# Splitting all four blocks of a treated K pair first, and rounding its three sums one by one on ScalarE

## The chip, the cores and the metric

The kernel runs on one core of one Trainium2 chip. The metric is the device time of one execution in microseconds. Before the change three runs took 2540.26, 2540.77 and 2540.88 us, median 2540.77.

## The reference

A decoder trunk of two layers on 256 rows of 2048 columns, in float32: a Mamba-2 mixer, then a SwiGLU feed-forward block (FFN), then differential attention, then a second FFN, with RMS norms around each. The change touches the FFNs alone:

```
def swiglu(h, w_gate, w_up, w_down):
    return (jax.nn.silu(h @ w_gate) * (h @ w_up)) @ w_down
...
D_FF = -(-8 * D_MODEL // (3 * 256)) * 256
```

So each FFN multiplies 256 x 2048 activations with two matrices of 2048 x 5632 and the product with one of 5632 x 2048.

## The kernel before

**Three products for one.** TensorE reads rounded operands (fp32r). To keep float32 accuracy each operand is split: `hi` is the value rounded (ScalarE, L133), `lo` is what the rounding left (VectorE, value minus `hi`, L134). A product is then three matmuls: hi by hi, hi by lo, lo by hi (L238).

**A pair of column blocks.** `pair` (L220) computes two neighbouring blocks of 512 columns for both halves of the rows (t = 0, 1). K runs in steps of 256 ("a K pair"): a step needs four weight blocks of 128 x 512, which SP loads into one tile `raw` (places 0, 1 of the first column block, 2, 3 of the second). A plain K pair takes 2 x 2 x 2 products, 24 matmuls. A *treated* K pair computes the same four 256 x 512 pieces with seven products in place of eight, after Winograd's form of Strassen's scheme, 21 matmuls. It needs seven right-hand operands: three weight blocks, one sum that GpSimd's accumulating DMA makes in place 0 (L247: it adds block 1 to it), and three sums that VectorE makes in place (L261 to L263). It also needs four differences of the activations, the "forms" (`make_form`, L820), which VectorE makes from the activations' two halves and which are split as well (`ff`).

**Products and where they go.** Three of the seven products belong to one output alone and accumulate in its PSUM bank `acc`, beside the plain K pairs' products; the other four ("p1", "p5", "p6", "p7") serve several outputs and accumulate in banks of the transposes' pool, `cp`. After the last treated K pair ScalarE and VectorE combine the `cp` banks (L276 to L280).

**Which K pairs.** In gate and up pairs K pairs 2, 4, 6 of 8 are treated, with a plain one between. In the down product `PARTS` names them. Each FFN has 39 treated K pairs. An FFN goes through its column pairs gate, up, gate, up, and now and then a pair of the down product, for the chunks of activations that are ready. After an up pair the activations (`s`, `sw`, `su`, `sx`: two chunks by two row halves) are scaled on VectorE (L897), transposed on TensorE (`pt_f`, L291) and split (`ah_f` on ScalarE, `al_f` on VectorE): the left-hand operands of the down product.

**What sets the order.** The program is recorded in the order of the code, with some work put off by `later`; a scheduler then orders each engine's instructions by what it reckons to be ready. On the chip each of ScalarE, VectorE and GpSimd does its own in that order. `hi` and `lo` come from rings of four tiles each (`hlB`): a tile is free again when the matmuls that read it are done. `raw` tiles come from a ring of three, in the middle part of an FFN from a second ring as well (`rawm`); a raw tile is free when its last low part is made, and only then does SP load the next block into it.

Of the kernel before, what the change touches and what calls it, by code (L numbers as in the profile page):

```python
# [41 lines left out]
def trunk_kernel(ctx, tc, x_rows, x_cols, vec_cols, vec64, post_rows, lam_rows,  # L42
                 w_zxbc, w_dt, w_so, w_qkv, w_ao,
                 w_g0, w_u0, w_d0, w_g1, w_u1, w_d1, out):
    nc = tc.nc
# [55 lines left out]
    xT_hi, xT_lo = [x[:, :, 0] for x in xT], [x[:, :, 1] for x in xT]  # L101
# [6 lines left out]
    hl = [hlA, 2]  # L108
    seq = [0]
# [5 lines left out]
    def raw_tile():  # L115
        deep[1] += 1
        if deep[0] and deep[1] % 5 in (1, 3):
            return mpool.tile([P, 4, 512], F32, tag="m", name="rawm")
        return rawp.tile([P, 4, 512], F32, tag="raw", name="raw")
# [6 lines left out]
    def prep(raw, scale=None):  # L126
        i = seq[0]
        seq[0] += 1
        w = raw.shape[1]
        hi = hl[0].tile([P, w, 512], F32R, tag="hi", name=f"hi{i}")  # L130
        lo = hl[0].tile([P, w, 512], F32R, tag="lo", name=f"lo{i}")
        if scale is None:
            nc.scalar.copy(hi, raw)  # L133
            nc.vector.tensor_tensor(lo, raw, hi.bitcast(F32), op=ALU.subtract)  # L134
        else:
            for j in range(w):
                nc.scalar.activation(hi[:, j], raw[:, j], AF.Copy, scale=scale[j])  # L137
                nc.vector.scalar_tensor_tensor(lo[:, j], raw[:, j], scale[j], hi[:, j].bitcast(F32),  # L138
                                               op0=ALU.mult, op1=ALU.subtract)
        return hi, lo  # L140
# [14 lines left out]
    def later(k, fn):  # L155
        at = step_no[0] + k
        i = len(deferred)
        while i and deferred[i - 1][0] > at:
            i -= 1
        deferred.insert(i, (at, fn))  # L160

    def tick():
        step_no[0] += 1
        while deferred and deferred[0][0] <= step_no[0]:
            deferred.pop(0)[1]()

# [53 lines left out]
    def pair(blocks, stat, seven, form, done):  # L220

        flush()
        acc = {}
        end = len(blocks) - 1  # L230

        def mm(k, st, hi, lo, last):
            first = k not in acc
            if first:
                acc[k] = (auxp.tile([P, 512], F32, tag="aux", name="cp") if isinstance(k, str) else
                          accp.tile([P, 512], F32, tag="acc", name="acc"))
            for q, (a, b) in enumerate(((st[0], hi), (st[0], lo), (st[1], hi))):
                nc.tensor.matmul(acc[k], a, b, start=first and q == 0, stop=last and q == 2)  # L238

        ss = {}  # L240
        for kp, src in enumerate(blocks):
            raw = raw_tile()
            for c in range(2):
                nc.sync.dma_start(raw[:, 2 * c:2 * c + 2], src[c])
            if kp in seven:

                nc.gpsimd.dma_start(raw[:, 0:1], src[0][:, 1:2], accum_op=ALU.add)  # L247
            if kp not in seven:
                hi, lo = prep(raw)
                for t in range(NT):  # L250
                    for c, e in ((0, 2), (1, 0)):
                        for j in range(2):
                            mm((t, c), stat(kp, j, t), hi[:, e + j], lo[:, e + j], kp == end and j == 1)
                        if kp == end:
                            done(t, c, acc[(t, c)], ss)
                    tick()
                continue
            last = kp == seven[-1]
            hi, lo = prep(raw[:, 1:4])

            nc.vector.tensor_tensor(raw[:, 2], raw[:, 2], raw[:, 0], op=ALU.add)  # L261
            nc.vector.tensor_tensor(raw[:, 3], raw[:, 3], raw[:, 2], op=ALU.add)
            nc.vector.tensor_tensor(raw[:, 1], raw[:, 2], raw[:, 1], op=ALU.subtract)  # L263
            sh, sl = prep(raw)
            mm("p1", stat(kp, 0, 0), hi[:, 1], lo[:, 1], last)
            mm((0, 0), stat(kp, 1, 0), hi[:, 2], lo[:, 2], False)
            mm((0, 1), form(kp, 3), hi[:, 0], lo[:, 0], False)
            tick()
            mm("p6", form(kp, 2), sh[:, 2], sl[:, 2], last)
            mm("p5", form(kp, 0), sh[:, 1], sl[:, 1], last)  # L270
            mm("p7", form(kp, 1), sh[:, 0], sl[:, 0], last)
            mm((1, 0), stat(kp, 1, 1), sh[:, 3], sl[:, 3], False)
            tick()
            if last:
                s1, u, w, x = (t512(n) for n in ("s1", "su", "sw", "sx"))
                nc.scalar.copy(s1, acc["p1"])  # L276
                nc.vector.tensor_tensor(u, acc["p6"], s1, op=ALU.subtract)
                nc.vector.tensor_tensor(w, acc["p5"], u, op=ALU.add)
                nc.vector.tensor_tensor(u, acc["p7"], u, op=ALU.add)
                nc.vector.tensor_tensor(x, acc["p7"], w, op=ALU.add)  # L280
                ss.update({(0, 0): (s1, ALU.add), (0, 1): (w, ALU.add), (1, 0): (u, ALU.subtract), (1, 1): (x, ALU.add)})

    def split(dst_hi, dst_lo, src):
        nc.scalar.copy(dst_hi, src)
        nc.vector.tensor_tensor(dst_lo, src, dst_hi.bitcast(F32), op=ALU.subtract)
# [46 lines left out]
    for k2 in range(KD // 2):  # L332
# [4 lines left out]
        if k2 < 6:  # L337
            if k2 % 2 == 0:
                z0_raw.append(rawp.tile([P, 4, 512], F32, tag="raw", name="raw"))
            ks = slice(k2 % 2 * 2, k2 % 2 * 2 + 2)  # L340
# [460 lines left out]
    def t512(name, shape=(P, 512)):  # L801
        return t5.tile(list(shape), F32, tag="t512", name=name)
# [14 lines left out]
    def xr_tile(name, shape=(P, 2, 512), dtype=F32):  # L817
        return postp.tile(list(shape), dtype, tag="xr", name=name, bufs=4)

    def make_form(dct, key, stat, t512, keep=None):  # L820

        xf = t512("xf", (P, NT, 2, P))
        f = t512("f", (P, 4, P))
        for t in range(NT):
            for j in range(2):
                hi, lo = stat(key, j, t)
                nc.vector.tensor_tensor(xf[:, t, j], hi.bitcast(F32), lo.bitcast(F32), op=ALU.add)
        nc.vector.tensor_tensor(f[:, 0], xf[:, 1, 0], xf[:, 1, 1], op=ALU.subtract)
        nc.vector.tensor_tensor(f[:, 1], xf[:, 1, 0], xf[:, 0, 0], op=ALU.subtract)
        nc.vector.tensor_tensor(f[:, 2], xf[:, 0, 0], f[:, 0], op=ALU.subtract)  # L830
        nc.vector.tensor_tensor(f[:, 3], xf[:, 0, 1], f[:, 2], op=ALU.subtract)
        ff = dct[key] = xr_tile("ff", (P, 4, 2, P), F32R)
        split(ff[:, :, 0], ff[:, :, 1], f)
        if keep:
            nc.sync.dma_start(keep, ff.rearrange("p f h q -> p (f h q)").bitcast(F32))

    def form_of(ff, f):
        return ff[:, f, 0], ff[:, f, 1]
# [19 lines left out]
    def ffn(wg, wu, wd, step, final):  # L858
        acts, gt, forms, keep, dforms = {}, {}, {}, {}, {}
# [13 lines left out]
        def kp_stat(kp, j, t):  # L873
            return x_stat(2 * kp + j, t)

        def kg_stat(kg, j, t):
            hi, lo = lookup(acts, (t, kg // 2))
            return hi[:, kg % 2 * 2 + j], lo[:, kg % 2 * 2 + j]

        def form(kp, f):  # L880
            return form_of(lookup(forms, kp), f)
# [29 lines left out]
                nc.sync.dma_start(xr_d[t][h].rearrange("p (e k) -> p e k", e=2), xr_of[(t, h)])  # L911
        for k, kp in enumerate(SEVEN):
            keep[kp] = dramp.tile([P, 8 * P], F32, name=f"form{step}_{kp}")
            later(1 + 3 * k, lambda kp=kp: make_form(forms, kp, kp_stat, t512, keep[kp]))
        mv([wu[10, k] for k in range(4)], u_stat, u_evac, LAG2)
        def form_later(k, kg):
            later(k, lambda: make_form(dforms, kg, kg_stat, t512))

# [4 lines left out]
        for pi, (part, kgs, two) in enumerate(PARTS):  # L923
# [17 lines left out]
            else:  # L941
# [5 lines left out]
                         mid=lambda: fetch_x(lambda t, h: xr_d[t][h].rearrange("p (e k) -> p e k", e=2)))  # L947

    ffn(w_g0, w_u0, w_d0, 1, False)


# [120 lines left out]
    for hg in range(4):  # L1072
        attention_group(hg)
    out_proj(w_ao, True, True, att, list(range(8)), 2, False, LAG2, t512, load_post(2))
    ffn(w_g1, w_u1, w_d1, 3, True)
    flush()

# [59 lines left out]
```

## Time and profile before

| stretch of the span, us | what runs | TensorE busy | VectorE busy | ScalarE busy | clock |
|---|---|---|---|---|---|
| 0 to 753 | Mamba mixer, start of FFN 1 | 747.2 | 528.1 | 467.5 | 1.00 |
| 753 to 1366 | FFN 1, paired columns | 612.9 | 512.2 | 308.6 | 1.00 |
| 1366 to 1869 | attention, start of FFN 2 | 501.1 | 321.1 | 263.5 | 1.00 |
| 1869 to 2482 | FFN 2, paired columns | 613.0 | 512.8 | 309.4 | 1.00 |
| 2482 to 2537 | last column block, norm, output | 43.5 | 28.4 | 15.7 | 0.93 |

The profiled execution took 2539.5 us, its span is 2537.7 us; the median of the three runs is 2540.77. Engines: PE is TensorE, PEld its weight loads, DVE VectorE, ACT ScalarE, POOL GpSimd, SP the engine that issues loads. L133 is line 133 of the kernel. A row of the timelines gives start and duration in us, engine, line, operation, output<-inputs, shapes, count, and in brackets the idle time before it with what ended it; a row of the groups gives count, busy time, mean ns of one, idle time before. The chain's rows give start, length and what ran.

### The profile page before, as it was taken

Reading aid. Unit: us, or ns where it says so; the run is one execution under the profiler, and the core shown is the slowest. Engines: PE = TensorE matmul, PEld = TensorE weight load, DVE = VectorE, ACT = ScalarE, POOL = GpSimd, SP = SyncE. Lnnn points to the kernel's source line nnn. Section 1 sums busy time; section 2 is a strip of 40 time slices with the busy share of each in tenths; the row PEclk is TensorE's granted clock in tenths of the full one; section 3 lists DMA queues with packets and bytes.
Section 4 is the critical chain, followed back from the end, with each engine's and each line's share of the span. In section 5 each row is a group of like instructions: output and inputs, shape, how many; then the busy total and the mean of one; then the engine's idle time right before and its main releaser. Section 6 shows DMA issues by size and latency. Waiting matters only on the chain.

```text
span 2537.7 us, 31211 instructions
## 1 busy us (share of the span) xinstructions
PE 2517.8 (99%) x11866; PEld 2072.2 (82%) x11866; DVE 1902.6 (75%) x2274; ACT 1364.7 (54%) x1655; POOL 222.4 (9%) x214
## 2 busy tenths in 40 slices
PE   9999999999999999999999999999999999999998
PEld 8877888788888888888888888887888888888886
DVE  6777547777687888977887765566688889878985
ACT  5767556666565454544454654455655454535453
POOL 0111000110110000001001100001100000010002
PEclk9999999999999999999999999999999999999999
DMA  7555555455776776778677544544666966786673
GB/s 287 190 169 182 189 191 198 166 183 177 254 260 210 253 238 210 236 231 243 210 237 246 189 150 166 183 151 156 241 223 201 294 216 208 235 262 213 205 252 146
DMA packets 141366, 536.16 MB, mean 211 GB/s; under 512 B 14176, under 2 KB 30880, under 8 KB 114208
## 3 DMA queue, kind: packets, MB, share of 16 engines
q1 hardware_dynamic: 125584, 502.91, 57.3%
q0 software_dynamic: 15264, 30.94, 6.5%
q8 instruction: 93, 1.52, 0.2%
q14 instruction: 57, 0.47, 0.0%
q10 hardware_dynamic: 368, 0.32, 0.0%
HBM read 516.22 MB, written 17.89 MB: 210 GB/s over the span
## 4 chain that ended last, share of the span: by engine, by line
PE 93%; DVE 2%; ACT 1%; issue 1%; DMA 1%; POOL 0%; SPq 0%; DVEq 0%; ACTq 0%; POOLq 0%
PE acc L238 38%; PE acc L187 34%; PE cp L238 8%; PE acc L212 5%; PE acc L214 2%; DVE lo L134 1%; PE sc L1013 1%; DMA mt<-acum_d 1%; PE pt_f L291 1%; ACT hi L133 1%; PE py L568 1%; PE ptx L661 0%; PE po L1049 0%; PE pc L475 0%; PE pp L1040 0%
## 5 line engine op out<-in xcount | busy, mean ns | idle before, releaser
L134 DVE TENSOR_TENSOR lo<-raw,hi 128x2048 fp32r<-128x2048 f32 (+2 forms) x451 | 848.6, 1888 | 362.4 <-ACT hi L133 353.2
L133 ACT CAST hi<-raw 128x2048 fp32r<-128x2048 f32 (+2 forms) x451 | 699.8, 1557 | 593.9 <-DVE raw L263 195.4
L238 PE MATMUL acc<-hi,xT 128*128 128x512 f32 x1840 | 589.2, 390 | 0.0
L187 PE MATMUL acc<-hi,xT 128*128 128x512 f32 x1792 | 588.9, 399 | 0.0
L238 PEld LDWEIGHTS acc<-hi,xT 128*128 128x128 f32 x1840 | 345.3, 188 | 71.5
L187 PEld LDWEIGHTS acc<-hi,xT 128*128 128x128 f32 x1792 | 335.9, 188 | 73.4 <-issue 4.9
L238 PE MATMUL acc<-lo,xT 128*128 128x512 f32 x920 | 358.1, 389 | 0.0
L187 PE MATMUL acc<-lo,xT 128*128 128x512 f32 x896 | 352.1, 393 | 1.1 <-DVE lo L134 1.1
L133 ACT CAST hi<-rawm 128x2048 fp32r<-128x2048 f32 (+1 forms) x115 | 207.8, 1807 | 173.4 <-DVE rawm L263 108.3
L134 DVE TENSOR_TENSOR lo<-rawm,hi 128x2048 fp32r<-128x2048 f32 (+1 forms) x115 | 248.0, 2157 | 69.9 <-ACT hi L133 66.1
L238 PEld LDWEIGHTS acc<-lo,xT 128*128 128x128 f32 x920 | 172.7, 188 | 35.5
L187 PEld LDWEIGHTS acc<-lo,xT 128*128 128x128 f32 x896 | 169.0, 189 | 38.0 <-DVE lo L134 3.6
L238 PE MATMUL acc<-hi,ah_f 128*128 128x512 f32 x468 | 183.1, 391 | 0.0
L238 PE MATMUL acc<-hi,al_f 128*128 128x512 f32 x468 | 182.1, 389 | 0.0
L238 PE MATMUL acc<-lo,ah_f 128*128 128x512 f32 x468 | 182.1, 389 | 0.0
L212 PE MATMUL acc<-xT,hi 128*128 128x512 f32 x512 | 179.8, 397 | 0.0
L238 PE MATMUL cp<-hi,ff 128*128 128x512 f32 x468 | 156.9, 389 | 0.0
L214 PE MATMUL acc<-xT,lo 128*128 128x256 f32 x512 | 142.6, 280 | 0.0
L138 DVE SCALAR_TENSOR_TENSOR lo<-raw,cols,hi 128x512 fp32r<-128x512 f32 x128 | 92.5, 767 | 57.2 <-ACT hi L137 56.9
L137 ACT ACTIVATE hi<-raw,cols 128x512 fp32r<-128x512 f32 x128 | 84.8, 715 | 58.9 <-PE acc L187 41.4
L212 PEld LDWEIGHTS acc<-xT,hi 128*128 128x128 f32 x512 | 96.1, 188 | 22.6
L238 PEld LDWEIGHTS acc<-hi,al_f 128*128 128x128 f32 x468 | 87.8, 188 | 18.4
(279 smaller groups left out, 3470.4 us busy)
## 6 DMA issues: line engine op xcount, KB each, us to landing
raw<-in_w_zxbc_dram SPq DMA_DIRECT2D x77, 1024.0 KB, 4.8
raw<-in_w_d_dram SPq DMA_DIRECT2D x98, 512.0 KB, 5.9
raw<-in_w_g_dram SPq DMA_DIRECT2D x96, 512.0 KB, 5.9
raw<-in_w_u_dram SPq DMA_DIRECT2D x96, 512.0 KB, 5.8
raw<-in_w_qkv_dram SPq DMA_DIRECT2D x48, 1024.0 KB, 4.8
raw<-in_w_so_dram SPq DMA_DIRECT2D x32, 1024.0 KB, 4.8
rawm<-in_w_g_dram SPq DMA_DIRECT2D x64, 512.0 KB, 5.8
rawm<-in_w_u_dram SPq DMA_DIRECT2D x64, 512.0 KB, 6.0
```

Of the source, the lines that this page charges most:

```text
L133: nc.scalar.copy(hi, raw)
L134: nc.vector.tensor_tensor(lo, raw, hi.bitcast(F32), op=ALU.subtract)
L137: nc.scalar.activation(hi[:, j], raw[:, j], AF.Copy, scale=scale[j])
L138: nc.vector.scalar_tensor_tensor(lo[:, j], raw[:, j], scale[j], hi[:, j].bitcast(F32), op0=ALU.mult, op1=ALU.subtract)
L187: nc.tensor.matmul(acc[t], a, b[:, j], start=(i == 0 and j == 0 and q == 0), stop=(i == last and j == 1 and q == 2))
L212: nc.tensor.matmul(acc[ct], hi[:, j, cs], x.rearrange("p a s -> p (a s)"), start=(i == 0 and j == 0), stop=False)
L214: nc.tensor.matmul(acc[ct][:, :S], lo[:, j, cs], x[:, 0], start=False, stop=(i == last and j == 1))
L238: nc.tensor.matmul(acc[k], a, b, start=first and q == 0, stop=last and q == 2)
L291: nc.tensor.transpose(pt[:, j], src[:, j * P:(j + 1) * P], ident)
L568: nc.tensor.matmul(py[e * 64:(e + 1) * 64, a], xd[c][:, 2 * a + e], mts[c][:, 2 * a + e], start=True, stop=True)
L1013: nc.tensor.matmul(sc[c][:, h], qT[cp, h % 2, ts], kT[cp, h % 2, :nk * P], start=True, stop=True)
```

## The change

In a treated K pair the first split now takes all four raw blocks, sum in place 0 included (before: places 1 to 3), and the second one only the three sums VectorE makes (before: all four places after the sums). ScalarE rounds each sum by an instruction of its own, right behind the VectorE instruction that makes it; the low parts of the three are made by two instructions, of two places and of one. The order of the sums changes with it, and the product "p7", whose operand now belongs to the first split, moves to the first group of matmuls: 12 matmuls read the first split and 9 the second (before 9 and 12). In `make_form` one addition per row half takes two blocks together (before: two additions).

```
-            hi, lo = prep(raw[:, 1:4])
+            hi, lo = prep(raw)
+            sh = hl[0].tile([P, 3, 512], F32R, tag="hi", name=f"sh{seq[0]}")
+            sl = hl[0].tile([P, 3, 512], F32R, tag="lo", name=f"sl{seq[0]}")
             nc.vector.tensor_tensor(raw[:, 2], raw[:, 2], raw[:, 0], op=ALU.add)
+            nc.scalar.copy(sh[:, 1], raw[:, 2])
+            nc.vector.tensor_tensor(raw[:, 1], raw[:, 2], raw[:, 1], op=ALU.subtract)
+            nc.scalar.copy(sh[:, 0], raw[:, 1])
             nc.vector.tensor_tensor(raw[:, 3], raw[:, 3], raw[:, 2], op=ALU.add)
-            nc.vector.tensor_tensor(raw[:, 1], raw[:, 2], raw[:, 1], op=ALU.subtract)
-            sh, sl = prep(raw)
-            mm("p1", stat(kp, 0, 0), hi[:, 1], lo[:, 1], last)
-            mm((0, 0), stat(kp, 1, 0), hi[:, 2], lo[:, 2], False)
-            mm((0, 1), form(kp, 3), hi[:, 0], lo[:, 0], False)
+            nc.scalar.copy(sh[:, 2], raw[:, 3])
+            nc.vector.tensor_tensor(sl[:, 0:2], raw[:, 1:3], sh[:, 0:2].bitcast(F32), op=ALU.subtract)
+            nc.vector.tensor_tensor(sl[:, 2], raw[:, 3], sh[:, 2].bitcast(F32), op=ALU.subtract)
+            mm("p1", stat(kp, 0, 0), hi[:, 2], lo[:, 2], last)
+            mm((0, 0), stat(kp, 1, 0), hi[:, 3], lo[:, 3], False)
+            mm((0, 1), form(kp, 3), hi[:, 1], lo[:, 1], False)
+            mm("p7", form(kp, 1), hi[:, 0], lo[:, 0], last)
             tick()
-            mm("p6", form(kp, 2), sh[:, 2], sl[:, 2], last)
-            mm("p5", form(kp, 0), sh[:, 1], sl[:, 1], last)
-            mm("p7", form(kp, 1), sh[:, 0], sl[:, 0], last)
-            mm((1, 0), stat(kp, 1, 1), sh[:, 3], sl[:, 3], False)
+            mm("p6", form(kp, 2), sh[:, 1], sl[:, 1], last)
+            mm("p5", form(kp, 0), sh[:, 0], sl[:, 0], last)
+            mm((1, 0), stat(kp, 1, 1), sh[:, 2], sl[:, 2], False)
             tick()
...
         for t in range(NT):
-            for j in range(2):
-                hi, lo = stat(key, j, t)
-                nc.vector.tensor_tensor(xf[:, t, j], hi.bitcast(F32), lo.bitcast(F32), op=ALU.add)
+            hi, lo = stat(key, t)
+            nc.vector.tensor_tensor(xf[:, t], hi.bitcast(F32), lo.bitcast(F32), op=ALU.add)
```

`kp_both` and `kg_both` return the two blocks of an activation that this addition takes. Lines behind the change move: L276 becomes L283, L291 L298, L897 L909, and `split`'s L284 and L285 become L291 and L292.

The order of the engines' instructions differs from the first treated block on. ScalarE, middle treated block of the third gate pair of FFN 1, before (`hi_8413` is the split of places 1 to 3, `hi_8420` the one of all four after the sums, `hi_8448` that of the next plain K pair):

```order
L133 CAST hi_8381<-rawm 128x2048
L133 CAST hi_8413<-raw 128x1536
L133 CAST hi_8420<-raw 128x2048
L133 CAST hi_8448<-raw 128x2048
L133 CAST hi_8480<-rawm 128x1536
```

The same after the change (`hi_8449` is the split of all four places, `sh_8453` the sums, `hi_8487` the next plain K pair):

```order
L133 CAST hi_8449<-raw 128x2048
L265 CAST sh_8453<-raw 128x512
L133 CAST hi_8487<-raw 128x2048
L267 CAST sh_8453<-raw 128x512
L269 CAST sh_8453<-raw 128x512
```

The next plain block's rounding stood behind the treated block's; now it stands between the first and the second of the sums' roundings.

ScalarE, first treated block of the down pair that follows the third up pair of FFN 1, before (`hi_8998` is the treated block's first split, `ah_f` are the transposed activations of chunks 5 and 4, `hi_9005` is the second split):

```order
L133 CAST hi_8966<-rawm 128x2048
L133 CAST hi_8998<-raw 128x1536
L284 CAST ah_f_5_0_8887<-pt_f_5_0_8882 128x512
L284 CAST ah_f_4_0_8896<-pt_f_4_0_8891 128x512
L284 CAST ah_f_5_1_8919<-pt_f_5_1_8914 128x512
L284 CAST ah_f_4_1_8928<-pt_f_4_1_8923 128x512
L133 CAST hi_9005<-raw 128x2048
```

After the change (`hi_9047` is the treated block's first split):

```order
L133 CAST hi_9015<-rawm 128x2048
L133 CAST hi_9047<-raw 128x2048
L291 CAST ah_f_5_0_8936<-pt_f_5_0_8931 128x512
L291 CAST ah_f_4_0_8945<-pt_f_4_0_8940 128x512
L291 CAST ah_f_5_1_8968<-pt_f_5_1_8963 128x512
L291 CAST ah_f_4_1_8977<-pt_f_4_1_8972 128x512
```

The places are the same, but the instruction ahead of `ah_f` now reads place 0 as well, which the accumulating DMA fills; before, that one was `hi_9005`, behind them.

VectorE at the same place, before (the scaling of the activations, `L897`, and the low parts of the transposed ones):

```order
L897 SCALAR_TENSOR_TENSOR su<-su,rs_pre_1_6345 128x512
L896 TENSOR_TENSOR sx<-acc,sx 128x512
L134 TENSOR_TENSOR lo_8936<-raw,hi_8935 128x2048
L897 SCALAR_TENSOR_TENSOR sx<-sx,rs_pre_1_6345 128x512
L285 TENSOR_TENSOR al_f_5_0_8888<-pt_f_5_0_8882,ah_f_5_0_8887 128x512
L285 TENSOR_TENSOR al_f_4_0_8897<-pt_f_4_0_8891,ah_f_4_0_8896 128x512
```

And after:

```order
L909 SCALAR_TENSOR_TENSOR su<-su,rs_pre_1_6345 128x512
L908 TENSOR_TENSOR sx<-acc,sx 128x512
L292 TENSOR_TENSOR al_f_5_0_8937<-pt_f_5_0_8931,ah_f_5_0_8936 128x512
L909 SCALAR_TENSOR_TENSOR sx<-sx,rs_pre_1_6345 128x512
L292 TENSOR_TENSOR al_f_4_0_8946<-pt_f_4_0_8940,ah_f_4_0_8945 128x512
```

The low part `lo_8936` has moved ahead of the whole scaling, and the first `al_f` now stands ahead of the scaling of `sx`. TensorE's order there is as before: the transposes of `su`, then those of `sx`, 12 matmuls behind those of `sw`.

More of the change, by code (lines that the diff above doesn't have):

```diff
@@ L874, in kp_stat, with kp_both, kg_both @@
             return x_stat(2 * kp + j, t)
-        def kg_stat(kg, j, t):
+        def kp_both(kp, t):
+            sl = slice(t * P, (t + 1) * P)
+            ks = slice(kp % 2 * 2, kp % 2 * 2 + 2)
+            return xT_hi[kp // 2][:, ks, sl], xT_lo[kp // 2][:, ks, sl]
+        def kg_both(kg, t):
             hi, lo = lookup(acts, (t, kg // 2))
-            return hi[:, kg % 2 * 2 + j], lo[:, kg % 2 * 2 + j]
+            return hi[:, kg % 2 * 2:kg % 2 * 2 + 2], lo[:, kg % 2 * 2:kg % 2 * 2 + 2]
         def form(kp, f):
@@ L913, in ffn @@
             keep[kp] = dramp.tile([P, 8 * P], F32, name=f"form{step}_{kp}")
-            later(1 + 3 * k, lambda kp=kp: make_form(forms, kp, kp_stat, t512, keep[kp]))
+            later(1 + 3 * k, lambda kp=kp: make_form(forms, kp, kp_both, t512, keep[kp]))
         mv([wu[10, k] for k in range(4)], u_stat, u_evac, LAG2)
         def form_later(k, kg):
-            later(k, lambda: make_form(dforms, kg, kg_stat, t512))
+            later(k, lambda: make_form(dforms, kg, kg_both, t512))
         md = [dramp.tile([P, D], F32, name=f"md{step}_{t}") for t in range(NT)]
```

## The prediction

> **What bounds the kernel now.** I read the page first, then the windows by stage, the chain of work, the waits of the weight loads, and last the timelines of the four engines at the places that the chain points to.
>
> ```profile
> span 2537.7 us, 31211 instructions
> PE 2517.8 (99%) x11866; PEld 2072.2 (82%) x11866; DVE 1902.6 (75%) x2274; ACT 1364.7 (54%) x1655; POOL 222.4 (9%) x214
> 753.00:1366.00 613.00, 612.93 (x2742) 507.27 (x2741) 512.24 (x486) 308.62 (x217) 42.36 (x51) 1.00 0.72 230
> 1869.00:2482.00 613.00, 612.97 (x2744) 507.40 (x2742) 512.82 (x486) 309.35 (x218) 42.88 (x51) 1.00 0.72 230
> ```
>
> The changed code runs only in the two FFN stretches, 753 to 1366 and 1869 to 2482. There TensorE shows no idle time at full clock (1.00), VectorE is busy 84% (512.24 of 613) and ScalarE 50%. So only a wait of TensorE can move the end. A busy matmul row can hide a short wait, because matmuls overlap; the chain shows it better, since its pieces begin where matmuls begin:
>
> ```profile
> 1041.35 6.12 PE acc L238 x27
> 1051.55 6.12 PE acc L238 x27
> ...
> 1253.68 6.12 PE acc L238 x27
> 1264.05 6.14 PE acc L238 x27
> 1274.62 17.01 PE acc L238 x75
> ...
> 2115.24 6.12 PE acc L238 x27
> 2125.61 6.14 PE acc L238 x27
> 2136.13 17.00 PE acc L238 x75
> ```
>
> Equal places of two neighbouring treated blocks stand 10.20 us apart when nothing waits (1051.55 - 1041.35): 21 matmuls of the treated block and 24 of the plain one between, 226.7 ns each. Here they stand 10.37 and 10.57 apart, then 10.37 and 10.52. The excess is 0.17 + 0.37 = 0.54 and 0.17 + 0.32 = 0.49 us. The weight loads name what was waited for:
>
> ```profile
> PEld cp L238 <- DVE lo L134: 2.9, 8, 0.5
> ```
>
> Eight waits for a low part: two in each of four gate pairs (two of these pairs are shown above). Four pairs at about 0.5 us make **2.0 us**, which is all that the treated blocks lose now.
>
> **The change, part by part.** Why those eight waits are there, by VectorE and ScalarE in the first such pair:
>
> ```profile
> 999.55 1.75 DVE L134 TENSOR_TENSOR lo<-raw,hi 128x1536 fp32r<-128x1536 f32 x1
> 1001.34 0.69 DVE L261 TENSOR_TENSOR raw<-raw 128x512 f32<-128x512 f32 x1
> 1002.07 0.69 DVE L262 TENSOR_TENSOR raw<-raw 128x512 f32<-128x512 f32 x1
> 1002.67 0.69 DVE L263 TENSOR_TENSOR raw<-raw 128x512 f32<-128x512 f32 x1
> 1005.47 4.49 DVE L134 TENSOR_TENSOR lo<-raw,hi 128x2048 fp32r<-128x2048 f32 x2 [2.11 <-ACT hi L133]
> 1009.88 1.75 DVE L134 TENSOR_TENSOR lo<-rawm,hi 128x1536 fp32r<-128x1536 f32 x1
> ```
>
> From one treated block's first low part to the next one's is 1009.88 - 999.55 = 10.33 us, of which 2.11 are idle: VectorE makes three sums, ScalarE rounds all four blocks, and only then comes the low part. 10.33 is more than TensorE's 10.20, so a pair that starts late stays late. The durations of the new order:
>
> ```profile
> L134 DVE TENSOR_TENSOR lo<-raw,hi 128x2048 fp32r<-128x2048 f32 x241 | 551.1, 2293 | 246.9 <-ACT hi L133 246.2
> L133 ACT CAST hi<-raw 128x2048 fp32r<-128x2048 f32 x241 | 458.6, 1911 | 411.2 <-DVE raw L263 195.4 <-PE acc L212 84.5 <-PE acc L187 37.8
> L134 DVE TENSOR_TENSOR lo<-raw,hi 128x1024 fp32r<-128x1024 f32 x160 | 210.7, 1321 | 96.6 <-ACT hi L133 88.1 <-PE pc L475 8.3
> L285 DVE TENSOR_TENSOR al_f<-pt_f,ah_f 128x512 fp32r<-128x512 f32 x44 | 28.4, 682 | 3.0 <-ACT ah_f L284 3.0
> L284 ACT CAST ah_f<-pt_f 128x512 fp32r<-128x512 f32 x44 | 23.8, 589 | 78.0 <-PE pt_f L291 78.0
> L827 DVE TENSOR_TENSOR xf<-ah_f,al_f 128x128 f32<-128x128 f32 x48 | 11.5, 282 | 0.1
> ```
>
> VectorE per treated block: before 1.75 + 3 x 0.69 + 2.29 = 6.11 us; after 2.29 + 3 x 0.69 + 1.32 + 0.69 = 6.37. So it works 0.26 longer; what goes is the idle 2.11. ScalarE: 1.91 and three roundings of about 0.6 in place of about 3.4, some 0.3 more, in an engine half idle.
>
> But the 2.11 doesn't go entirely. In the built order ScalarE does the next plain block's rounding (1.91) between the first and the second small one. From the start of the low part of four: 2.3 to its end, 0.7 for the first sum, about 0.7 for the first small rounding, 1.8 for the plain block's (starts of queued instructions lie some 0.1 closer than durations), 0.6 for the second small one; then 1.3 and 0.6 for the two low parts, and 2.2 for the plain block's. That is 10.2 at most, about 0.1 under the present 10.33, and TensorE's own period. What gains more is the sums' deadline: seven products need the first split less one, so the sums' group now starts after 12 matmuls, not 9, and may come 3 x 0.227 = 0.68 us later, and their low part is done about 1 us earlier than the four-block one (before the plain block's low part). I take all eight waits as gone: **-2.0**; the ends are 0 (the plain block, at 10.2, becomes the late one) and -2.9 (the whole row of weight-load waits).
>
> Forms: VectorE saves about 48 x 0.28 less 24 longer adds, some 3 us over both FFNs with the copies from xT; TensorE waits for none of it, so 0. If its cover (the lead of the forms) were gone it would be part of the 2.0 above.
>
> **What the first split now waits for.** Block 0 is filled in by GpSimd's accumulating DMA. Until now only the first sum waited for it; now ScalarE's big rounding does, and ScalarE works in order. One place shows what that means already now, with a load:
>
> ```profile
> 1326.12 1.48 ACT L133 CAST hi<-raw 128x1536 fp32r<-128x1536 f32 x1 [5.06 <-DMA raw<-in_w_d_dram]
> 1327.51 1.06 ACT L284 CAST ah_f<-pt_f 128x512 fp32r<-128x512 f32 x2
> ```
>
> Elsewhere the accumulation is early; in the pair above its DMA was issued 15.7 us ahead of the rounding:
>
> ```profile
> 981.06 0.86 POOL L247 DMA_DIRECT2D raw<-in_w_g_dram  x1 [10.16 <-DMA raw<-in_w_g_dram]
> ...
> 996.76 1.48 ACT L133 CAST hi<-raw 128x1536 fp32r<-128x1536 f32 x1
> ```
>
> Not in the first treated block of the down pair after the third pair of columns, where the transposed activations' roundings stand behind it:
>
> ```profile
> 1063.74 0.88 POOL L247 DMA_DIRECT2D raw<-in_w_d_dram  x1 [1.14 <-DMA raw<-in_w_d_dram]
> ...
> raw<-in_w_d_dram POOLq DMA_DIRECT2D x1, 256.0 KB, 9.2
> ...
> 1067.90 1.49 ACT L133 CAST hi<-raw 128x1536 fp32r<-128x1536 f32 x1 [3.21 <-PE acc L238]
> 1071.07 1.07 ACT L284 CAST ah_f<-pt_f 128x512 fp32r<-128x512 f32 x2 [1.68 <-PE pt_f L291]
> ...
> 1072.59 0.74 DVE L897 SCALAR_TENSOR_TENSOR sx<-sx,rs_pre 128x512 f32<-128x512 f32 x1
> ...
> 1074.48 0.60 PE L291 MATMUL pt_f<-ident,sx 128*128 128x128 f32 x4
> ```
>
> It lands at 1063.74 + 9.2 = 1072.9. The rounding of four, now from 1072.9, frees ScalarE at 1074.8; `ah_f` of chunk 5 ends at 1075.4, its `al_f` on VectorE at 1076.1. In the new order `sx` is scaled behind that `al_f` (now ahead of it, at 1072.59): 1076.8. TensorE's transposes of `sx` stand at 1074.48, with the next block's matmuls behind them in its order: 2.3 us. Since the raw tile whose release starts this load comes free about 0.4 earlier (the low parts end earlier), I take **+1.9**. The second FFN has the same place:
>
> ```profile
> 2179.98 0.89 POOL L247 DMA_DIRECT2D raw<-in_w_d_dram  x1 [1.52 <-DMA raw<-in_w_d_dram]
> ...
> raw<-in_w_d_dram POOLq DMA_DIRECT2D x1, 256.0 KB, 8.4
> ...
> 2190.34 0.60 PE L291 MATMUL pt_f<-ident,sx 128*128 128x128 f32 x4
> ```
>
> Landed 2188.4, plus 1.9 + 0.55 + 0.7 + 0.7 = 2192.2, against 2190.34: 1.9, less 0.4 is **+1.5**. Bounds: 0 each, if the accumulation lands two microseconds sooner, and 2.3 + 1.9 = 4.2, if no sooner. In the same down pair and in the next, one low part (2.2 us) moves ahead of the scaling that the transposes need; by the same steps the transposes are then met within 0.2 us, so I take 0, with 0 to 0.7 at four places kept for the range.
>
> [...] The 226.7 ns above hold for plain blocks as well, at clock 1.00, and no row here shows a closer spacing; the measurement decides.
>
> **Sum.** -2.0 + 1.9 + 1.5 + 0 = +1.4 us. The profiled execution took 2539.5 (span 2537.7 and 1.8 around it), so 2540.9 by it; the median of the three runs is 1.3 higher, 2540.77, so 2542.2. A measurement here tells about 0.2%, 5.1 us, from no change.
>
> **Rivals.** *The accumulation is early enough* (the first tile comes free sooner, or the DMA engines are less crowded): then only the gain is left, 2540.77 - 2.0 = 2538.8. For it: all traffic there follows releases that come earlier; against it: 9.2 and 8.4 us at both of these places. 25%.
> *Slower: ScalarE's queue held by a later accumulation.* Freed tiles start loads earlier, and these compete with the accumulation; 2 us later at both places makes -2.0 + 4.2 + 4.0 = +6.2, 2547.0. It decides from a landing later than about 1070.6 (1072.9 - 2.3) in the first FFN: from there each microsecond is one of TensorE's. 17%, 7 of them with at least the 5.1 us.
> *The change doesn't do what it says*: with the plain block's rounding in between, the eight waits only move to its low part, and the two new ones come on top: +3.4, 2544.2. 7%.
> [...]
>
> **Numbers.** My case, 50%, reaches from 2540.8 to 2543.5. The range from 2538.4 to 2545.0 takes in the early landing and half of the slow case. Slower by over 0.2% (above 2545.9) are the 7% of the slow rival; faster by over 0.2% (below 2535.7) has the page's rule and what I overlook, 2%; within 0.2%: 91%.
>
> **What would show it.** Right: no weight load of a `cp` matmul waits for a low part in the gate pairs, steps of 10.20 there; transposes L298 of `sx` waiting some 1 to 2 us near 1074 and 2190; ScalarE idle before the four-block rounding there with the accumulating DMA as releaser. Wrong: gaps that stay at 10.37, a transposed piece on time, or waits elsewhere, such as a weight load for an accumulator not yet emptied.

## The result, and the profile after

The changed kernel took **2559.6 us** (median of six runs, 2553.6 to 2560.2), the kernel before 2540.1 beside it (six runs, 2539.7 to 2540.9): a ratio of 1.0074, with a 95% interval of 1.0064 to 1.0084. That is 19 us slower, far above the forecast 2542.2 and its range. The profiled execution took 2559.66 us, its span is 2557.9.

First the page of the changed kernel: the span, the engines' busy time, and the chain of work that ended last, by engine and by line.

```profile
span 2557.9 us, 31384 instructions
...
PE 2524.4 (99%) x11866; PEld 2076.1 (81%) x11866; DVE 1909.3 (75%) x2316; ACT 1385.7 (54%) x1811; POOL 222.3 (9%) x214
...
PE 83%; DMA 5%; DVE 5%; ACT 3%; issue 2%; POOL 0%; SPq 0%; DVEq 0%; ACTq 0%; POOLq 0%
```

TensorE is still "99% busy" and has the same 11866 matmuls. The chain says more: a part of the span that belonged to TensorE (93% before, with 1% DMA, 2% VectorE and 1% ScalarE) is now with DMA, VectorE and ScalarE. The rows of TensorE's waits name what it stood for (engine, line, what was waited for: us in total, times, longest):

```profile
PE acc L238 <- DVE sw L727: 4.8, 4, 1.7
PE acc L238 <- ACT ah_f L291: 4.0, 2, 2.2
PE pt_f L298 <- DVE sx L909: 2.8, 2, 1.9
...
PE pt_f L298 <- DVE g L876: 1.1, 1, 1.1
```

None of these waits is there before. What is gone is the row of the weight loads of `cp` that waited for a low part (2.9 us, eight times), on which the forecast gain rested.

Both programs have their matmuls in nearly the same order, so the start of the matmul at the same place of that order can be compared. How much later it starts after the change than before grows at these places (by the times after; a subtraction from the matmul rows of both traces):

| us, after | what begins there | adds, us |
| --- | --- | --- |
| 865-877 | second column pair of a down pair | 2.0 |
| 1072-1086 | down pair after the third pair of columns | 3.8 |
| 1156-1169 | gate pair after that down pair | 1.6 |
| 1339-1378 | last down pair of the first FFN | 4.8 |
| 1875-1895 | first gate pair of the second FFN | 1.4 |
| 1995-2008 | twin of 865 | 1.4 |
| 2192-2206 | twin of 1072 | 1.2 |
| 2278-2290 | twin of 1156 | 1.0 |
| 2457-2472 | twin of 1339 | 4.0 |
| 2485-2511 | end of that down pair | 0.9 |

Together 22.1 us; 20.2 is the difference of the spans (2557.9 - 2537.7), so some 2 us were won elsewhere. The gain is where it was forecast, at the four gate pairs that lost time before: past the third of them the same matmuls start 14.01 us later than before ahead of it and 13.52 behind it, past the fourth 15.78 and 15.28. The four steps are 0.52, 0.55, 0.49 and 0.50, 2.06 us in all.

**The first place.** ScalarE, GpSimd and VectorE of the changed kernel where the second column pair of the first down pair begins:

```profile
857.83 0.86 POOL L247 DMA_DIRECT2D raw<-in_w_d_dram  x1 [34.16 <-DMA rawm<-in_w_d_dram]
...
866.03 1.91 ACT L133 CAST hi<-raw 128x2048 fp32r<-128x2048 f32 x1 [6.48 <-DMA raw<-in_w_d_dram]
...
864.43 0.69 DVE L727 TENSOR_TENSOR s<-acc,s 128x512 f32<-128x512 f32 x1 [0.66 <-PE acc L238]
867.97 2.29 DVE L134 TENSOR_TENSOR lo<-raw,hi 128x2048 fp32r<-128x2048 f32 x1 [2.85 <-ACT hi L133]
870.18 0.68 DVE L292 TENSOR_TENSOR ff<-f,ff 128x512 fp32r<-128x512 f32 x1
870.78 0.68 DVE L727 TENSOR_TENSOR sw<-acc,sw 128x512 f32<-128x512 f32 x1
...
871.52 0.50 PE L238 MATMUL acc<-hi,ah_f 128*128 128x512 f32 x1 [1.69 <-DVE sw L727]
```

Its DMA issues, in a window around 857.83 (KB, us to landing):

```profile
raw<-in_w_d_dram POOLq DMA_DIRECT2D x1, 256.0 KB, 8.0
```

The accumulating DMA was issued at 857.83 and landed 8.0 us later, at 865.8. ScalarE had been idle for 6.48 us and could start the rounding only then. VectorE had the low part of that rounding **ahead of the evacuations of the accumulators** in its order, so it stood idle too (2.85 us), and the evacuations (L727) came at 870.78. TensorE needed the accumulator at 869.8. The same place before:

```profile
857.75 0.86 POOL L247 DMA_DIRECT2D raw<-in_w_d_dram  x1 [34.53 <-DMA rawm<-in_w_d_dram]
...
raw<-in_w_d_dram POOLq DMA_DIRECT2D x1, 256.0 KB, 7.6
...
862.96 1.49 ACT L133 CAST hi<-raw 128x1536 fp32r<-128x1536 f32 x1 [3.52 <-PE acc L238]
...
864.32 0.69 DVE L720 TENSOR_TENSOR s<-acc,s 128x512 f32<-128x512 f32 x1 [0.46 <-PE acc L238]
...
865.60 1.75 DVE L134 TENSOR_TENSOR lo<-raw,hi 128x1536 fp32r<-128x1536 f32 x1
867.27 0.68 DVE L720 TENSOR_TENSOR sw<-acc,sw 128x512 f32<-128x512 f32 x1
```

The low part stood ahead of those evacuations before the change too. It did no harm there: three blocks don't need the accumulation, the rounding began at 862.96, 2.4 us before the DMA landed (857.75 + 7.6 = 865.3).

**The place that was forecast**, at 1074, by the same engines:

```profile
1074.34 1.91 ACT L133 CAST hi<-raw 128x2048 fp32r<-128x2048 f32 x1 [8.39 <-DMA raw<-in_w_d_dram]
1076.15 1.54 ACT L291 CAST ah_f<-pt_f 128x512 fp32r<-128x512 f32 x3
...
1076.76 0.69 DVE L292 TENSOR_TENSOR al_f<-pt_f,ah_f 128x512 fp32r<-128x512 f32 x1 [3.52 <-ACT ah_f L291]
1077.36 0.74 DVE L909 SCALAR_TENSOR_TENSOR sx<-sx,rs_pre 128x512 f32<-128x512 f32 x1
...
1078.16 0.66 PE L298 MATMUL pt_f<-ident,sx 128*128 128x128 f32 x4 [1.88 <-DVE sx L909]
1078.58 0.48 PE L238 MATMUL acc<-hi,ah_f 128*128 128x512 f32 x1
1078.89 0.47 PE L238 MATMUL acc<-lo,ah_f 128*128 128x512 f32 x1
1079.16 0.63 PE L238 MATMUL acc<-hi,al_f 128*128 128x512 f32 x1
1079.59 0.63 PE L238 MATMUL acc<-hi,ah_f 128*128 128x512 f32 x1
```

The rounding waits for the DMA, `ah_f` stands behind it, `al_f` behind that, and `sx` behind the first `al_f`: TensorE waits 1.88 us, where 1.9 was forecast. Then comes something that wasn't: the matmuls that follow soon start 0.43 us apart, not 0.23. The windows give the granted clock there (start:end, length, busy us and count of PE, PEld, DVE, ACT and POOL, clock, DMA share, GB/s):

```profile
1079.00:1082.50 3.50, 3.50 (x10) 2.72 (x9) 3.50 (x4) 0.44 (x1) 0.00 (x0) 0.51 0.13 32
1344.50:1348.00 3.50, 3.50 (x10) 2.79 (x11) 3.46 (x4) 0.08 (x1) 0.00 (x0) 0.62 0.13 23
2469.00:2471.40 2.40, 2.40 (x6) 1.88 (x6) 2.40 (x3) 0.00 (x0) 0.00 (x0) 0.50 0.21 37
```

The granted clock is about one half here, behind three of the waits. In the three stretches 8, 8 and 5 matmuls start 0.43 us apart instead of 0.23: 21 x 0.2 = 4.2 us, time in which TensorE counts as busy.

**The largest place**, the last down pair of the first FFN:

```profile
1330.84 0.86 POOL L247 DMA_DIRECT2D raw<-in_w_d_dram  x1 [32.89 <-DVE su L908]
...
1340.73 1.90 ACT L133 CAST hi<-raw 128x2048 fp32r<-128x2048 f32 x1 [14.15 <-DMA raw<-in_w_d_dram]
1342.54 2.04 ACT L291 CAST ah_f<-pt_f 128x512 fp32r<-128x512 f32 x4
...
1343.65 0.50 PE L238 MATMUL acc<-hi,ah_f 128*128 128x512 f32 x1 [2.22 <-ACT ah_f L291]
```

and the DMA issue at 1330.84:

```profile
raw<-in_w_d_dram POOLq DMA_DIRECT2D x1, 256.0 KB, 9.7
```

All four `ah_f` stand behind a rounding ahead of which ScalarE stood idle for 14.15 us. Before, the accumulation of this block landed 5.1 us after its issue:

```profile
1325.46 0.87 POOL L247 DMA_DIRECT2D raw<-in_w_d_dram  x1 [34.28 <-DVE sx L896]
...
raw<-in_w_d_dram POOLq DMA_DIRECT2D x1, 256.0 KB, 5.1
```

Now it took 9.7. SyncE's loads show what else was under way, after and then before:

```profile
1323.48 3.13 SPq L244 DMA_DIRECT2D raw<-in_w_d_dram  x3
...
1329.72 0.43 SPq L244 DMA_DIRECT2D raw<-in_w_d_dram  x1
1330.24 0.38 SPq L850 DMA_DIRECT2D x<-xr_d  x1
```

```profile
1318.69 0.80 SPq L244 DMA_DIRECT2D raw<-in_w_d_dram  x2
...
1327.06 5.41 SPq L244 DMA_DIRECT2D raw<-in_w_d_dram  x4
```

The block's own two loads are the first two of each. After the change the next tile's first load goes out within 3 us of them, and its second one 1 us ahead of the accumulation; before, these came 8 us later and 1.6 us behind the accumulation's issue.

### The profile page after: what moved, and what is told of

It is laid out like the page before. It is cut to its first block, busy times and chain, and to the rows that moved or that the text cites. A ratio compares the mean times of both kernels' runs of the same rounds, so it can differ in the third digit from the quotient of the medians.

```text
span 2557.9 us, 31384 instructions
## 1 busy us (share of the span) xinstructions
PE 2524.4 (99%) x11866; PEld 2076.1 (81%) x11866; DVE 1909.3 (75%) x2316; ACT 1385.7 (54%) x1811; POOL 222.3 (9%) x214
## 4 chain that ended last, share of the span: by engine, by line
PE 83%; DMA 5%; DVE 5%; ACT 3%; issue 2%; POOL 0%; SPq 0%; DVEq 0%; ACTq 0%; POOLq 0%
PE acc L187 33%; PE acc L238 31%; PE cp L238 7%; PE acc L212 5%; DVE lo L134 3%; DMA raw<-in_w_d_dram 2%; PE acc L214 2%; ACT hi L133 1%; DMA raw<-in_w_g_dram 1%; DMA rawm<-in_w_d_dram 1%; PE sc L1025 1%; DMA mt<-acum_d 1%; PE py L575 1%; PE pt_f L298 1%; PE ptx L668 0%
## 5 line engine op out<-in xcount | busy, mean ns | idle before, releaser
L134 DVE TENSOR_TENSOR lo<-raw,hi 128x2048 fp32r<-128x2048 f32 (+1 forms) x401 | 762.7, 1906 | 290.2 <-ACT hi L133 281.0
L133 ACT CAST hi<-raw 128x2048 fp32r<-128x2048 f32 (+1 forms) x401 | 628.2, 1567 | 428.2 <-PE acc L187 152.2
L187 PE MATMUL acc<-hi,xT 128*128 128x512 f32 x1792 | 589.5, 400 | 0.0
L238 PE MATMUL acc<-hi,xT 128*128 128x512 f32 x1720 | 553.4, 390 | 2.0 <-DVE sw L727 2.0
L187 PEld LDWEIGHTS acc<-hi,xT 128*128 128x128 f32 x1792 | 336.1, 188 | 73.0 <-issue 4.9
L238 PEld LDWEIGHTS acc<-hi,xT 128*128 128x128 f32 x1720 | 323.0, 188 | 69.3 <-DVE sw L727 2.8
L187 PE MATMUL acc<-lo,xT 128*128 128x512 f32 x896 | 352.3, 394 | 1.0 <-DVE lo L134 1.0
L238 PE MATMUL acc<-lo,xT 128*128 128x512 f32 x860 | 334.9, 389 | 0.0
L134 DVE TENSOR_TENSOR lo<-rawm,hi 128x2048 fp32r<-128x2048 f32 x87 | 199.1, 2288 | 34.3 <-ACT hi L133 29.8
L133 ACT CAST hi<-rawm 128x2048 fp32r<-128x2048 f32 x87 | 166.4, 1913 | 75.3 <-PE acc L238 33.6
L187 PEld LDWEIGHTS acc<-lo,xT 128*128 128x128 f32 x896 | 169.1, 189 | 37.9 <-DVE lo L134 3.4
L238 PEld LDWEIGHTS acc<-lo,xT 128*128 128x128 f32 x860 | 161.5, 188 | 33.2
L238 PE MATMUL acc<-hi,ah_f 128*128 128x512 f32 x450 | 179.1, 398 | 6.8 <-ACT ah_f L291 4.0
L238 PE MATMUL acc<-hi,al_f 128*128 128x512 f32 x450 | 177.8, 395 | 0.1
L238 PE MATMUL acc<-lo,ah_f 128*128 128x512 f32 x450 | 177.3, 394 | 0.0
L265 ACT CAST sh<-raw 128x512 fp32r<-128x512 f32 x50 | 31.1, 622 | 179.9 <-DVE raw L264 176.2
L270 DVE TENSOR_TENSOR sl<-raw,sh 128x1024 fp32r<-128x1024 f32 x50 | 61.3, 1226 | 65.7 <-ACT sh L267 64.8
```

What stands on the lines that cost most here:

```text
L187: nc.tensor.matmul(acc[t], a, b[:, j], start=(i == 0 and j == 0 and q == 0), stop=(i == last and j == 1 and q == 2))
L265: nc.scalar.copy(sh[:, 1], raw[:, 2])
L270: nc.vector.tensor_tensor(sl[:, 0:2], raw[:, 1:3], sh[:, 0:2].bitcast(F32), op=ALU.subtract)
```

## The experiments

**Theory A**: the first rounding now waits for the accumulating DMA, and what is queued behind it on ScalarE, and behind its low part on VectorE, comes late. **Rival B**: the sums, rounded in three pieces, make low parts late. **Rival C**: the merged additions in the forms reorder the queues. Four runs take the change apart (medians of 8 to 10 executions; before 2540.7 us beside them).

*Place 0 rounded by itself.*

```
-            hi, lo = prep(raw)
+            hi, lo = prep(raw[:, 1:4])
...
+            nc.scalar.copy(sh[:, 3], raw[:, 0])
+            nc.vector.tensor_tensor(sl[:, 3], raw[:, 0], sh[:, 3].bitcast(F32), op=ALU.subtract)
```

> The changed kernel, but the first rounding leaves out place 0, the one that the accumulating DMA fills; place 0 has a rounding and a low part of its own behind the sums, and its product goes back to the second group. Theory A (the loss is work queued behind an instruction that waits for the accumulating DMA): the low part of three places no longer waits, so the four TensorE waits on accumulators behind it (4.8 us by the profile after) vanish; the order built for ScalarE still has place 0's own rounding ahead of the transposed activations' roundings, so the waits there (4.0 + 2.8 us, and the stretches at half spacing behind them) stay: 2546 to 2553 us. Rival B (the small roundings between the sums make the low parts late): nothing changes, 2557 to 2561. Rival C (the merged form instructions reorder the queues): the same, 2557 to 2561.

Measured: **2539.0 us**, ratio 0.9993 (0.9984 to 1.0003). None of the four waits is left. That is theory A's direction, but outside the 2546 to 2553 that I gave it, and better. I had misread the order at the place near 1340: place 0's rounding stands between the second and the third `ah_f` there, and the first two, which TensorE needs first, don't wait.

```profile
1323.03 1.48 ACT L133 CAST hi<-raw 128x1536 fp32r<-128x1536 f32 x1 [4.75 <-DMA raw<-in_w_d_dram]
1324.97 1.07 ACT L293 CAST ah_f<-pt_f 128x512 fp32r<-128x512 f32 x2 [0.45 <-PE pt_f L300]
1329.21 0.62 ACT L272 CAST sh<-raw 128x512 fp32r<-128x512 f32 x1 [3.17 <-DMA raw<-in_w_d_dram]
1329.74 1.06 ACT L293 CAST ah_f<-pt_f 128x512 fp32r<-128x512 f32 x2
```

*Place 0 rounded together with the last sum.*

```
-            hi, lo = prep(raw)
+            hi, lo = prep(raw[:, 1:4])
...
-            nc.scalar.copy(sh[:, 2], raw[:, 3])
+            nc.scalar.copy(sh[:, 2:4], raw[:, 0:4:3])
```

> The changed kernel, but place 0 is rounded together with the last sum, so that nothing of it can stand ahead of the sums; the first rounding takes three places, as before the change, and its product p7 goes back to the second group. The three sums are still rounded one by one and the forms still merged. Theory A: every wait behind the accumulating DMA goes, only the gain of about 2.0 us is left: 2537 to 2540 us. Rival B or C: the loss stays, 2555 us or more.

Measured: **2538.5 us**, ratio 0.9993 (0.9983 to 1.0002). The pieces and the merged forms are still in it, so neither makes the loss. Rivals B and C fall as single causes. Nor is a late landing enough by itself. The same three accumulations that land late in the changed kernel's last down pairs and near 1875 take 9.8, 10.0 and 9.7 us here, near 1322, 1856 and 2437, and no matmul waits for them. The first of them:

```profile
1322.38 0.86 POOL L247 DMA_DIRECT2D raw<-in_w_d_dram  x1 [33.50 <-DVE sw L908]
...
raw<-in_w_d_dram POOLq DMA_DIRECT2D x1, 256.0 KB, 9.8
```

*The kernel before, with four places rounded first.*

```
-            hi, lo = prep(raw[:, 1:4])
+            hi, lo = prep(raw)
...
-            sh, sl = prep(raw)
+            sh, sl = prep(raw[:, 1:4])
```

> The kernel before, with one thing of the change: the first rounding takes all four places and the second the three sums, in one instruction each as before; p7 is made of the first. Theory A: the loss comes with this alone, 2555 to 2563 us (no gain of 2.0 in it, since the sums are still rounded in one piece). Rival B or C: 2539 to 2542 us.

Measured: **2546.1 us** (2544.0 to 2550.3), ratio 1.0024 (1.0014 to 1.0035). The direction is that of theory A, but it is a miss of its range: under a third of the loss. Its waits are mostly those for evacuations, and none is for `ah_f` or `sx`. (The profile is of the slowest of the eight executions, 2550.3 us.)

```profile
PE acc L238 <- DVE sw L720: 5.3, 4, 2.7
PE cp L238 <- DVE lo L134: 2.2, 3, 1.0
```

*The merged forms alone, in the kernel before.*

```
-            for j in range(2):
-                hi, lo = stat(key, j, t)
-                nc.vector.tensor_tensor(xf[:, t, j], hi.bitcast(F32), lo.bitcast(F32), op=ALU.add)
+            hi, lo = stat(key, t)
+            nc.vector.tensor_tensor(xf[:, t], hi.bitcast(F32), lo.bitcast(F32), op=ALU.add)
```

> The kernel before, with only the merged additions in the forms. Theory A: 2539.5 to 2541 us, no change. Rival C (the merged forms shift the order built for VectorE and cost waits): a large part of the 19.5 us, 2545 us or more.

Measured: 2541.2 us, ratio 0.9999 (0.9990 to 1.0009). By themselves the forms cost nothing.

**Is it the wait, or the order?** The next pair leaves the DMA out and keeps the rest. Without it the changed kernel's ScalarE order is the same by the traces, row by row; VectorE's and TensorE's differ in 4 rows each.

```
-                nc.gpsimd.dma_start(raw[:, 0:1], src[0][:, 1:2], accum_op=ALU.add)
+                pass
```

> The changed kernel without the accumulating DMA: place 0 keeps the first block alone, so the second block's part of p7 and of the sums is left out, and 0.25 MB less is moved per treated block. Theory A (work queued behind instructions that wait for this DMA): all of the loss goes, and 2535 to 2539 us are left. Rival B (the roundings in pieces make low parts late by themselves): 2553 us or more.

> The kernel before without the accumulating DMA, the same work left out: what its bytes alone are worth where only the first sum waits for it. Theory A: 2538 to 2541 us, within 2 us of before. A fall by 5 us or more would say that the run of the changed kernel without it is faster for the bytes and not for the wait.

Measured: the changed kernel **2535.6 us**, the kernel before **2537.2**. So taking the DMA away gives the changed kernel 24.0 us and the kernel before 3.5 (2540.6 to 2537.2, a little more than I had allowed for the bytes). The difference, 20.5 us, is what waiting for it costs, all of the loss, and what is left of the change is a gain of 1.6. This is the plainest result of the series.

**At which blocks?** Nine places in the table, all but its last row, lie at the first treated block of a pair. (The expectation below calls the one near 1880 a second block; by the trace it is the first too: in the run that treats the first blocks apart, the rounding there takes three places, at 1865.25.) Two runs split the 78 treated blocks: in one the first of each pair is done as in the run with place 0 in the last sum, in the other all but the first (the two branches change places).

```
+            if kp == seven[0]:
+                hi, lo = prep(raw[:, 1:4])
...
+                nc.scalar.copy(sh[:, 2:4], raw[:, 0:4:3])
...
+            else:
+                hi, lo = prep(raw)
...
+                nc.scalar.copy(sh[:, 2], raw[:, 3])
```

> The changed kernel, but the first treated block of each pair is done as in the run with place 0 rounded with the last sum; all other treated blocks stay as changed. If the loss sits only where a pair begins and its first accumulation lands late (eight of the nine places that lost time), it goes but for the one place that is a second block (near 1880 us in the profile after, 1.7 us): 2538 to 2543 us. If every treated block adds to it: 2550 us or more.

> The other way round: the first treated block of each pair as changed, all others with place 0 rounded with the last sum. If the loss sits at the first blocks: 2550 to 2561 us. If every treated block adds to it: 2546 us or less.

Measured: **2539.0 us** (0.9983 to 1.0002) with the first blocks freed, **2557.2** (1.0051 to 1.0081) with only the first blocks as changed. No wait near 1880 is left in the first of these runs. The loss sits at the first blocks, 30 of 78.

**Why only 5 us with four rounded first in the kernel before?** Theory A2: the pieces add the rest, through the order that they bring and the tiles that they free.

*One rounding and one low part of three for the sums.*

```
-            nc.scalar.copy(sh[:, 1], raw[:, 2])
...
-            nc.scalar.copy(sh[:, 2], raw[:, 3])
+            nc.scalar.copy(sh, raw[:, 1:4])
...
+            nc.vector.tensor_tensor(sl, raw[:, 1:4], sh.bitcast(F32), op=ALU.subtract)
```

> The changed kernel with its sums rounded in one instruction of three places and one low part of three, as before the change; the first rounding of four, p7 in the first group and the merged forms stay. It differs from the kernel of before with four rounded first (2546.1 us) only in the order of the sums and in the forms. Theory A2 (the wait alone costs about 6 us; the pieces add the rest, since with them VectorE's built order puts al_f ahead of the scaling of sx, and freed tiles start loads that delay the accumulation in the last down pairs): 2544 to 2549 us, no transposes waiting for sx. Rival D (what lies between 2546 and 2559.6 comes from p7 in the first group, the order of the sums or the merged forms): 2555 us or more.

Measured: **2555.4 us** (2552.1 to 2557.6): a miss, on rival D's side; p7's place is one more difference from the run at 2546.1. No transposes wait for `sx` any more, as expected, but other waits grew:

```profile
PE acc L238 <- DVE sw L724: 6.1, 4, 2.8
PE acc L238 <- ACT ah_f L288: 2.3, 1, 2.3
```

So the pieces aren't what the early loads near 1325 need: they go out here too (third load 2.8 us behind the block's own first one), and the accumulation took 9.7 us again.

*One low part of three behind the three small roundings.*

```
-            nc.vector.tensor_tensor(sl[:, 0:2], raw[:, 1:3], sh[:, 0:2].bitcast(F32), op=ALU.subtract)
-            nc.vector.tensor_tensor(sl[:, 2], raw[:, 3], sh[:, 2].bitcast(F32), op=ALU.subtract)
+            nc.vector.tensor_tensor(sl, raw[:, 1:4], sh.bitcast(F32), op=ALU.subtract)
```

> The changed kernel with the sums rounded in three pieces but with one low part of three places behind them, so that a raw tile comes free about a microsecond later. Its order still has al_f ahead of the scaling of sx. Theory A2: the waits for sx (2.8 us) stay, with their stretches at half spacing; if the early freed tile is what delays the accumulation in the last down pairs, the two waits for ah_f (4.0 us) and the half spacing behind them shrink: 2549 to 2556 us. If the order of the roundings alone makes them, 2557 to 2561.

Measured: **2573.5 us**, a miss of 17 us. The parts that I named came as said: the accumulation near 1340 landed 5.5 us after its issue, no wait for `ah_f` is left, the ones for `sx` stay. But the order built for this program is another one on TensorE too, and has a wait of its own, matmuls of `cp` for a first rounding that is held:

```profile
PE cp L238 <- ACT hi L133: 6.2, 2, 4.0
PE acc L238 <- DVE sw L726: 5.5, 4, 1.9
PE pt_f L297 <- DVE sx L908: 5.0, 2, 2.6
```

*p7 back in the second group, with one rounding of the sums; and the merged forms on the kernel before with four first.* These look for the 9 us between 2546.1 and 2555.4 in one of the differences. The second is the diff of the forms above, on the run with four places first; the first moves one line:

```
-            mm("p7", form(kp, 1), hi[:, 0], lo[:, 0], last)
             tick()
...
             mm("p5", form(kp, 0), sh[:, 0], sl[:, 0], last)
+            mm("p7", form(kp, 1), hi[:, 0], lo[:, 0], last)
```

> The run with the sums rounded in one piece (2555.4 us), with p7 back in the second group of products. The kernel of before with four rounded first (2546.1 us) has p7 there too. If p7 in the first group (its products wait for the accumulated place, in TensorE's order ahead of the sums' products) carries the 9 us between these two: 2545 to 2548 us. If the order of the sums or of the queues does: 2553 to 2557 us.

> The kernel before with four rounded first (2546.1 us) and the merged forms. The forms alone cost nothing in the kernel before. If the 9 us come with the forms once a rounding waits (they move VectorE's order in 104 of some 2,000 rows): 2552 us or more. If not: 2544 to 2548 us.

Measured: **2550.4 us** (seven executions, 2544.4 to 2554.6) and **2549.3** (six, 2546.7 to 2551.6). Both lie between the two answers that I had put down: neither part carries the 9 us. Put in a row, the runs with the wait in them go from 2546.1 (four rounded first) by 2549.3 (and the merged forms), 2550.4 (and the order of the sums) and 2555.4 (and p7 in the first group) to 2559.6 (and the sums in pieces): each part adds something, p7 and the pieces most, but the intervals of neighbours overlap, so no single step is shown. Executions of one such kernel can also lie far apart: 10 us in the run at 2550.4, where the kernel before beside it has 1.4; the run at 2573.5 has only 1.3. All six variants, beside the changed kernel itself, in which the first blocks' first rounding waits for the DMA are slower than before, by 5 to 33 us.

## Why the prediction was wrong

**What bounds the kernel, and the gain.** Right. Only a wait of TensorE moved the end; the eight waits are gone and were worth about 2 us: 2.06 by the matmuls' starts in the two traces, 1.6 by the pair without the DMA, 1.7 to 2.2 by the medians of the three versions that free the first blocks (each for itself within its interval of no change).

**The spacing of 226.7 ns.** It stayed: the closest that 45 matmuls of 512 columns (L238) follow each other is 226.6 ns in the mean, in the trace of before and of after. A part of the 2% for a faster result, and the last 1% of the chances, stood for a closer spacing; no run shows one.

**"Elsewhere the accumulation is early."** This sentence is the step that failed. I drew it from one row, an accumulation issued 15.7 us ahead of its rounding in the middle of a gate pair. The trace of before holds the answer for all 78 blocks: take the landing (issue row plus time to landing) from the start of the 128x1536 rounding. In 11 blocks the rounding began before the accumulation had landed:

| 128x1536 rounding, before | landed | short by, us |
| --- | --- | --- |
| 862.96 | 865.33 | 2.4 |
| 1067.90 | 1072.89 | 5.0 |
| 1111.85 | 1113.35 | 1.5 |
| 1148.57 | 1150.40 | 1.8 |
| 1326.12 | 1330.56 | 4.4 |
| 1340.42 | 1342.69 | 2.3 |
| 1978.85 | 1981.45 | 2.6 |
| 2183.77 | 2188.37 | 4.6 |
| 2227.72 | 2229.09 | 1.4 |
| 2264.44 | 2267.23 | 2.8 |
| 2441.53 | 2445.55 | 4.0 |

Eight of these eleven are where the changed kernel loses. I priced the two at 1067.90 and 2183.77 and saw the landing nowhere else. The prediction even quotes the rounding at 1326.12, which then waited for a load, and doesn't ask for the accumulation of the same block, issued at 1325.46 and landed at 1330.56. The ninth place, near 1875, couldn't be seen this way: its accumulation had 2.6 us to spare before (landing 1861.98, rounding 1864.61), and took 9.7 us after the change instead of 5.0.

**Who stands behind the waiting instruction.** I followed ScalarE's queue, and VectorE's only at the places of `sx`. At four places the loss runs through VectorE: the low part of four stands ahead of the evacuations, and TensorE waits for accumulators (4.8 us). The list of what would show the forecast wrong named an accumulator not yet emptied, without a price.

**The price at the two places.** At 1074 a wait of 1.9 us was forecast and 1.88 came, by the path that was described. At 2190 it was 1.5 against 0.9 measured. The forecast took 0.4 off for an earlier landing at both; measured against TensorE's own place, the landings came 0.3 and 0.9 us earlier. What the sum lacked was the half clock behind the wait at 1074, 1.6 us.

**The slow rival**, ScalarE's queue held by a later accumulation because freed tiles load earlier, had 17%, was bound to the same two places, and gave 2547.0. The queue held by the accumulation is what happened, and at nine places. The reason given for it fits only three of them: near 1340, 1875 and 2465 the accumulation landed 3.8 to 4.2 us later than before, measured against TensorE's own place. At the other six it landed at most 1.2 us later, and at four of these earlier; it had come that late before, when only VectorE's first sum waited for it. The rival's chance and the range came out of the same unchecked sentence.

What stays open: how the size depends on the built order. Built orders of nearly the same work gave 5 to 33 us, and no part of the change alone explains the steps between; I have not found which instruction frees the next tile earlier near 1325. The clock was only watched, not varied by itself. It may be what spreads the executions of one program: in the run at 2550.4, the two with a mean granted clock of 0.999 took 2544.4 and 2545.1 us, the five at 0.997 or 0.998 took 2549.6 to 2554.6.

## What to carry to other kernels

When an edit lets an instruction read something that arrives later than its other inputs, subtract arrival from start for **every** instance in the old trace, not for one; and look at the first block of each stage, where the queues here held the previous stage's results (the evacuations on VectorE, the `ah_f` on ScalarE). Then list what stands behind the instruction on its own engine, and behind its consumers on theirs. Here the loss goes when the late place is left out of the first rounding, as it was before the change, at the first blocks at least (2538.5 to 2539.0 us in three versions); the 2 us of gain that these medians keep are not told from no change by their intervals.

## What the hardware showed

**Behind most waits of 2 us and more the clock was halved.** Over the traces of all 14 kernels, in the two FFN stretches, I compared each stall of TensorE (start to start, less the usual spacing) with the spacing that follows within 7 us. Of 27 stalls between 0.8 and 1.91 us (one more fell into such a stretch) none was followed by matmuls 0.43 us apart; of 16 between 1.95 and 4.2 us, 14 were, 4 to 12 matmuls each (two stalls, 2.11 and 2.47 us, were not; why is not shown). Eight such matmuls take 3.4 us and lose 1.6. So a wait of some 2 us here can cost nearly twice its length: near 1074 it was 2.04 us so counted (1.88 by the row's idle time), with 1.6 lost behind it. In the changed kernel's trace the granted clock stands at one half from 1079.07, 1345.31 and 2468.30 us on, for 3.41 us each.

**The accumulating DMA landed in 3.9 to 10.2 us.** In the trace of before, the 256 KB of one block took 3.95 to 4.4 us in 36 of 78 blocks; in 35 of these no more than one load of 512 KB was under way when it was issued. In the 30 that took 6.9 to 9.2 us, 1 MB or more of other transfers was. After the change the shortest took 3.9 and the longest 10.2; the first block of the first FFN's last down pair took 5.1 us before and 9.7 after.
